# Causal mask of a stick-breaking attention: from an added matmul to the scan's second operand

## The chip, the cores and the metric

The kernel runs on one core of a Trainium2 chip. The metric is the device time of one execution, in microseconds (us); lower is better. A core has five engines, each with its own instruction stream: PE (TensorE, matrix products; its weight loads are listed as PEld), DVE (VectorE), ACT (ScalarE), POOL (GpSimd) and SP (SyncE, which issues most transfers). Each engine works through its own list in order, and an instruction whose operand is not ready holds up all that stand behind it on that engine.

## The reference, cut to what matters

One decoder block on 1024 positions of width 1024. A combined projection feeds three groups of heads (a short convolution, attention, a gated MLP over chunks); their outputs go through an output projection, a squared-ReLU MLP of width 4096 and a gate. The change touches the attention alone: eight heads of width 64, in blocks of 128 queries.

```python
for qb in range(s_len // Q_BLOCK):
    z = jnp.einsum('bqhd,bkhd->bhqk', qi, kj) * scale
    causal = s_pos < t_pos
    log_beta = jax.nn.log_sigmoid(z)
    log_rem = jnp.where(causal, jax.nn.log_sigmoid(-z), 0.0)
    suffix = lax.cumsum(log_rem, axis=3, reverse=True) - log_rem
    weights = jnp.where(causal, jnp.exp(log_beta + suffix), 0.0)
    o = jnp.einsum('bhqk,bkhd->bqhd', weights, vj)
```

With r = sigmoid(-z), and with r taken as 1 at a masked key, the weight of key s is the product of r over the keys after s, less that product taken from s on. So a kernel needs one running product from the last key to the first, and differences of neighbours. A masked key must leave the product at 1.

## The kernel before, in words

Every fp32 product is made of three reduced-precision products. `split` makes a high part (ACT, L138, or L141 with a scale) and a low part (DVE, L139, or L142 with a scale) of an operand, and `product` adds hi·hi, hi·lo and lo·hi in one PSUM bank (L165 to L167).

In the order of PE the block is: the projection of the gated MLP (to 74 us); projection of query, key and value of head pair 0 (`qkv_ps`); attention of head pairs 0 to 3, from 108 us, woven with other work; the output projection (`o_ps`, from 416 us); the MLP up (`f_ps`, from 501 us) and down (`d_ps`, from 816 us); the gate (`g_ps`, to 1205 us).

Attention of a head pair has 8 steps (two heads `hh`, four groups `g` of two query blocks `t`), each in two parts:

- `stick(hh, g)`, for each of two blocks `t` with `W = (t+1)*128` keys: for each half of up to 512 keys, PE makes logits `z` from the queries `QS` by the high and the low part of the keys (`KH` L447, `KL` L449); ACT writes `rem`, the sigmoid of minus the scaled logit (L454). Then DVE runs one scan over the whole row from the last key to the first, in place (L458), and `wt`, the difference of neighbours, is made at L464: on DVE for t = 3, 5, 7, on POOL for the others.
- `gather(hh, g)`: PE transposes `wt` in blocks into `w_tr` (L486), ACT and DVE split it (`wT_hi`, `wT_lo`), PE multiplies by the values `V` into `av` (L504).

In the half that holds the diagonal a third matmul (L453) adds to `z` a constant tile `below`, multiplied by the identity: 0 where the key lies before the query, -2^60 elsewhere. The sigmoid of a masked logit is then 1.

```python
back = rem[:, :W][:, ::-1]
nc.vector.tensor_tensor_scan(out=back, data0=back, data1=back, initial=1.0,
                             op0=ALU.mult, op1=ALU.bypass)
```

The list of steps is written out so that `stick` of the next step comes ahead of `gather` of this one. Both are generators that yield counts (shares of PE work), and `weave` takes from two streams so that their counts grow in proportion: attention of pair `pr` with total `ATTEND`, and, as filler, the projection of pair `pr+1` (`project`) or, with the last pair, the short convolution (`cv_ps`). A projection makes `qkv_ps`, scales query and key (`qk`, L382), and writes `V` (L141, L142). Every second block of queries and keys is then transposed (`turn_qk`: the bank `qk_tr`, L401), and from `qk_tr` come `QS`, its low part `q_lo`, `KH` and, on DVE, two pieces of `KL` (L407). The banks `qk_tr` and `w_tr` come from one pool, `ps_tr`, so a transpose waits until an earlier bank of the pool has been read. After this the framework's scheduler orders each engine's instructions anew, from a timeline that it simulates when it builds the program.

Of the kernel before, what the change touches and what calls it, by code (L numbers as in the profile page):

```python
# [6 lines left out]

F32 = mybir.dt.float32
F32R = mybir.dt.float32r
AF = mybir.ActivationFunctionType  # L10
ALU = mybir.AluOpType
AX = mybir.AxisListType

P = 128
T = 1024
# [17 lines left out]
def hybrid_block(ctx: ExitStack, tc: tile.TileContext, a: dict):  # L33
# [5 lines left out]
    nc = tc.nc  # L39
    PSUM = bass.MemoryType.PSUM  # L40

    const = ctx.enter_context(tc.tile_pool(name="const", bufs=1))
# [61 lines left out]
    for _ in range(WARM):  # L104
        nc.tensor.matmul(warm[:, :P], ones, ones, start=True, stop=True)
    ident_r = const.tile([P, P], F32R, name="ident")
# [1 line left out]
    nc.gpsimd.memset(ident, 0.0)  # L108
    nc.gpsimd.affine_select(out=ident_r, in_=ident, pattern=[[-1, P]], base=0,
                            channel_multiplier=1, compare_op=ALU.not_equal, fill=1.0)  # L110

    below = const.tile([P, P], F32R, name="below")
    nc.gpsimd.memset(below.bitcast(F32), 0.0)
    nc.gpsimd.affine_select(out=below, in_=below.bitcast(F32), pattern=[[-1, P]], base=0,
                            channel_multiplier=1, compare_op=ALU.is_gt, fill=-2.0 ** 60)
    mhalf = const.tile([P, 8], F32, name="mhalf")
    nc.gpsimd.memset(mhalf, -0.5)

# [115 lines left out]
    attn_scope = ExitStack()  # L234
    at = attn_scope.enter_context(tc.tile_pool(name="at", bufs=2))
    lo_p, hi_p = slice(0, HD), slice(HD, P)

# [181 lines left out]
    def attend(pr):  # L421

        QS, KH, KL, V, _ = heads[pr]
        yb = y_kept if pr == 3 else None
        if pr == 3:
            y_kept.extend(halves("y_b"))
        weights, both, seen_g = {}, [None], []

        def store_rows():

            while len(summed) > (0 if pr == 3 else 1):
                to, t = summed.pop(0)
                nc.sync.dma_start(to, t[:HD])

        def stick(hh, g):
            weights[hh, g] = []
            for t in (2 * g, 2 * g + 1):
                W = (t + 1) * P
                th, ts = block(t)

                rem = at.tile([P, T], F32, tag="rem", name=name("rem"), bufs=3)
                wt = at.tile([P, T], F32, tag="wt", name=name("wt"), bufs=4)
                for kh in reversed(range(th + 1)):
                    n = min(HT, W - kh * HT)
                    ks = slice(kh * HT, kh * HT + n)
                    z = bank(ps_z, "z")[:, :n]
                    nc.tensor.matmul(z, QS[hh][th][:, ts], KH[hh][kh][:, :n],  # L447
                                     start=True, stop=False)
                    nc.tensor.matmul(z, QS[hh][th][:, ts], KL[hh][kh][:, :n],  # L449
                                     start=False, stop=kh < th)  # L450
                    if kh == th:

                        nc.tensor.matmul(z[:, n - P:], ident_r, below, start=False, stop=True)  # L453
                    last_act[0] = nc.scalar.activation(rem[:, ks], z, AF.Sigmoid,  # L454
                                                       scale=-HD ** -0.5)

                back = rem[:, :W][:, ::-1]
                nc.vector.tensor_tensor_scan(out=back, data0=back, data1=back, initial=1.0,  # L458
                                             op0=ALU.mult, op1=ALU.bypass)


                on_vector = t in (3, 5, 7)
                nc.gpsimd.memset(wt[:, W - 1:W], 0.0)
                done = (nc.vector if on_vector else nc.gpsimd).tensor_tensor(  # L464
                    out=wt[:, :W - 1], in0=rem[:, 1:W], in1=rem[:, :W - 1], op=ALU.subtract)
                if not on_vector:
                    last_pool[0] = done
                weights[hh, g].append(wt)
                yield 2 * (t + 1) + 10

        def gather(hh, g):
            own = slice(hh * HD, (hh + 1) * HD)
            wts = weights.pop((hh, g))
            av_of[0] ^= 1
            av = av_bank[:, av_of[0] * 256:(av_of[0] + 1) * 256]

            def turn(j):

                tr = bank(ps_tr, "w_tr")
                n = 0  # L480
                parts = []
                for kb in (2 * j, 2 * j + 1):
                    first = 0 if kb <= 2 * g else 1
                    parts.append((kb, n, first))
                    for i in range(first, 2):
                        nc.tensor.transpose(tr[:, n:n + P], wts[i][:, kb * P:(kb + 1) * P], ident)  # L486
                        n += P
                hi, lo = tmp("wT_hi", F32R), tmp("wT_lo", F32R)
                split(tr[:, :n], hi[:, :n], lo[:, :n])
                return parts, hi, lo, n // P  # L490

            turned = []
            for j in range(-2, g + 1):
                if j + 2 <= g:
                    turned.append(turn(j + 2))
                    yield 2 * turned[-1][3] + 10
                if j < 0:
                    continue
                parts, hi, lo, _ = turned.pop(0)
                for kb, o, first in parts:  # L500
                    m = 256 - first * P
                    lhs = V[kb // 2][:, kb % 2, hh].rearrange("p two d -> p (two d)")
                    for part in (hi, lo):
                        nc.tensor.matmul(av[:, first * P:], lhs, part[:, o:o + m],  # L504
                                         start=kb == 0 and part is hi,
                                         stop=kb == 2 * g + 1 and part is lo)
                yield 8

            if yb is None:
                if both[0] is None:  # L510
                    both[0] = slot("y_both")
                t = both[0]
                nc.scalar.copy(t[:, (g % 2) * 256:(g % 2 + 1) * 256], av)
                if len(seen_g) % 2:
                    nc.gpsimd.dma_start(t[:HD], t[HD:], accum_op=ALU.add)
                    summed.append((y_dram[pr, g // 2, own], t))
                    both[0] = None
                seen_g.append(g)
                return
            low = half_tmp("av_lo")  # L520
            nc.scalar.copy(low[:HD], av[HD:])
            nc.vector.tensor_tensor(out=yb[g // 2][own, (g % 2) * 256:(g % 2 + 1) * 256],
                                    in0=av[:HD], in1=low[:HD], op=ALU.add)

        return stick, gather, store_rows

    def attention():
# [19 lines left out]
                yield None  # L547

    AHEAD = 26
    ATTEND = 2 * (72 + 8 * 10 + 72 + 10 * 10 + 80)  # L550


    gs_b = const.tile([P, 256], F32, name="gs_b")
# [144 lines left out]
    fill = stream(project(1), project(2), project(3), convolve())  # L698
# [139 lines left out]
    for q in range(FT):  # L838
        base = 7 * (q - 1)
# [85 lines left out]
    for h in range(2):  # L925
        for n in (0, 4, 1, 5, 2, 6, 3, 7):
# [28 lines left out]
            t = hg[n][h] = late_slot("tmp", "hg")  # L955
# [184 lines left out]
    for s, (c, p, j) in enumerate(steps):  # L1140
# [13 lines left out]
        elif p == 6:  # L1154
            subtract(nc.vector, u_sum[j], u_sum[j], bank)
            if last:
                add(nc.vector, h_res[j][1], h_res[j][1], u_sum[j])
                for h in range(2):
                    t = residual(j + 4, h)
# [185 lines left out]
```

## Time and profile before

| | |
|---|---|
| median of 3 runs | 1213.11 us (1210.53 to 1213.97) |
| the profiled execution | 1212.77 us, its span 1211.1 us |
| granted TensorE clock | 0.995 |
| PE busy | 1188.3 us (98%) |
| DVE busy | 885.2 us (73%) |
| ACT busy | 595.8 us (49%) |
| POOL busy | 405.0 us (33%) |
| mask matmuls (L453) | 64, in the attention |
| scans (L458) | 64, 90.6 us on DVE |

The span is the time from the first to the last instruction, 1.7 us less than the time of that execution. A row of a group of instructions reads: line, engine, operation, output<-inputs, shapes, count, then busy us and mean ns of one, then the engine's idle time just before them and what ended it. A row of the timeline reads: start, length, engine, line, operation, count, and in brackets the idle time ahead with what released it. PE matmuls are pipelined: one begins while the one before it drains, so what a matmul takes from PE is the time from its start to the next start, not its listed length.

### The profile page before, as it was taken

Reading aid. Unit: us, or ns where it says so; the run is one execution under the profiler, and the core shown is the slowest. Engines: PE = TensorE matmul, PEld = TensorE weight load, DVE = VectorE, ACT = ScalarE, POOL = GpSimd, SP = SyncE. Lnnn points to the kernel's source line nnn. Section 1 sums busy time; section 2 is a strip of 40 time slices with the busy share of each in tenths; the row PEclk is TensorE's granted clock in tenths of the full one; section 3 lists DMA queues with packets and bytes.
Section 4 is the critical chain, followed back from the end, with each engine's and each line's share of the span. In section 5 each row is a group of like instructions: output and inputs, shape, how many; then the busy total and the mean of one; then the engine's idle time right before and its main releaser. Section 6 shows DMA issues by size and latency. Waiting matters only on the chain.

```text
span 1211.1 us, 17645 instructions
## 1 busy us (share of the span) xinstructions
PE 1188.3 (98%) x5852; PEld 1015.5 (84%) x5852; DVE 885.2 (73%) x1310; ACT 595.8 (49%) x1148; POOL 405.0 (33%) x472
## 2 busy tenths in 40 slices
PE   9999999999999999999999999999999999999997
PEld 7899899899878888888888888888888888888886
DVE  7846788989887667877877777787665656753597
ACT  7735555565643356734333343355443444546542
POOL 2324435465453312034453544421023301013412
PEclk9999999999999999999999999999999999999999
DMA  9602349989654776779998999677889975644857
GB/s 317 225 18 106 112 152 277 251 176 186 144 117 100 179 265 207 214 189 267 264 251 241 251 244 263 213 258 271 307 261 307 284 260 172 221 155 114 177 162 208
DMA packets 127964, 254.04 MB, mean 210 GB/s; under 512 B 14496, under 2 KB 22432, under 8 KB 127168
## 3 DMA queue, kind: packets, MB, share of 16 engines
q1 hardware_dynamic: 94992, 168.08, 41.5%
q0 software_dynamic: 27664, 57.05, 25.2%
q10 hardware_dynamic: 5216, 27.79, 6.3%
q8 instruction: 46, 0.75, 0.3%
q14 instruction: 46, 0.38, 0.1%
HBM read 192.30 MB, written 92.80 MB: 235 GB/s over the span
## 4 chain that ended last, share of the span: by engine, by line
PE 85%; DVE 7%; DMA 4%; issue 2%; ACT 1%; POOL 0%; ACTq 0%; SPq 0%; DVEq 0%; POOLq 0%
PE f_ps L814 25%; PE d_ps L814 25%; PE g_ps L814 6%; PE qkv_ps L165 3%; PE qkv_ps L166 3%; PE qkv_ps L167 3%; DVE rem L458 2%; PE av L504 2%; PE w_tr L486 2%; PE vu_ps L167 1%; PE vu_ps L165 1%; PE vu_ps L166 1%; PE o_ps L167 1%; PE o_ps L165 1%; PE o_ps L166 1%
## 5 line engine op out<-in xcount | busy, mean ns | idle before, releaser
L139 DVE TENSOR_TENSOR w_lo<-raw,w_hi 128x512 fp32r<-128x512 f32 x280 | 240.8, 864 | 87.4 <-ACT w_hi L138 85.5
L138 ACT CAST w_hi<-raw 128x512 fp32r<-128x512 f32 x280 | 172.0, 619 | 241.1 <-PE d_ps L814 121.0
L814 PE MATMUL f_ps<-hn_hi,w_hi 128*128 128x512 f32 x448 | 175.1, 392 | 0.0
L814 PE MATMUL f_ps<-hn_hi,w_lo 128*128 128x512 f32 x448 | 174.9, 391 | 0.0
L814 PE MATMUL f_ps<-hn_lo,w_hi 128*128 128x512 f32 x448 | 174.8, 390 | 0.0
L814 PE MATMUL d_ps<-f_hi,w_hi 128*128 128x512 f32 x448 | 174.8, 390 | 0.0
L814 PE MATMUL d_ps<-f_hi,w_lo 128*128 128x512 f32 x448 | 174.3, 389 | 0.0
L814 PE MATMUL d_ps<-f_lo,w_hi 128*128 128x512 f32 x448 | 174.3, 389 | 0.0
L458 DVE TENSOR_TENSOR_SCAN rem<-rem 128x128 f32<-128x128 f32 (+3 forms) x64 | 90.6, 1426 | 19.3 <-ACT rem L454 19.2
L814 PEld LDWEIGHTS f_ps<-hn_hi,w_hi 128*128 128x128 f32 x448 | 84.5, 189 | 17.8 <-issue 0.2
L814 PEld LDWEIGHTS f_ps<-hn_lo,w_hi 128*128 128x128 f32 x448 | 84.5, 189 | 17.7 <-issue 0.2
L814 PEld LDWEIGHTS f_ps<-hn_hi,w_lo 128*128 128x128 f32 x448 | 84.4, 188 | 17.8
L814 PEld LDWEIGHTS d_ps<-f_lo,w_hi 128*128 128x128 f32 x448 | 84.1, 188 | 17.8 <-issue 0.2
L814 PEld LDWEIGHTS d_ps<-f_hi,w_hi 128*128 128x128 f32 x448 | 84.1, 188 | 17.6 <-issue 0.2
L814 PEld LDWEIGHTS d_ps<-f_hi,w_lo 128*128 128x128 f32 x448 | 84.1, 188 | 17.5
L165 PE MATMUL qkv_ps<-whi,xn_hi 128*128 128x384 f32 x256 | 89.7, 350 | 1.1 <-DVE V L142 1.1
L167 PE MATMUL qkv_ps<-whi,xn_lo 128*128 128x384 f32 x256 | 87.6, 342 | 0.0
L166 PE MATMUL qkv_ps<-wlo,xn_hi 128*128 128x384 f32 x256 | 87.4, 341 | 0.0
L139 DVE TENSOR_TENSOR f_lo<-raw,f_hi 128x512 fp32r<-128x512 f32 x112 | 77.1, 718 | 9.6 <-ACT f_hi L138 9.3
L800 POOL TENSOR_TENSOR S<-S,sq 128x512 f32<-128x512 f32 x19 | 27.4, 1441 | 157.8 <-ACT sq L876 157.8
L138 ACT CAST f_hi<-raw 128x512 fp32r<-128x512 f32 x112 | 67.0, 620 | 23.3 <-DMA raw<-f_dram 20.0
L454 ACT ACTIVATE rem<-z 128x128 f32<-128x128 f32 (+3 forms) x96 | 46.4, 500 | 33.0 <-PE z L453 19.2
(252 smaller groups left out, 2656.2 us busy)
## 6 DMA issues: line engine op xcount, KB each, us to landing
raw<-in_w_ff SPq DMA_DIRECT2D x148, 256.0 KB, 4.0
raw<-f_dram SPq DMA_DIRECT2D x112, 256.0 KB, 4.9
raw<-w_sums SPq DMA_DIRECT2D x64, 256.0 KB, 4.1
f_dram<-f SPq DMA_DIRECT2D x48, 256.0 KB, 4.1
f_dram<-t SPq DMA_DIRECT2D x48, 256.0 KB, 3.8
w_sums<-in_w_ff POOLq DMA_DIRECT2D x8, 1024.0 KB, 12.5
w_sums<-w_sums POOLq DMA_DIRECT2D x8, 1024.0 KB, 13.1
raw<-in_w_out SPq DMA_DIRECT2D x28, 256.0 KB, 3.3
```

Source lines behind the costliest of these rows:

```text
L138: last_hi[0] = nc.scalar.copy(hi, src)
L139: low.tensor_tensor(out=lo, in0=src, in1=hi, op=ALU.subtract)
L165: nc.tensor.matmul(ps, lh, rh, start=first and i == 0, stop=False)
L166: nc.tensor.matmul(ps, lh, rl, start=False, stop=False)
L167: done = nc.tensor.matmul(ps, ll, rh, start=False, stop=last and i == len(terms) - 1)
L454: last_act[0] = nc.scalar.activation(rem[:, ks], z, AF.Sigmoid, scale=-HD ** -0.5)
L458: nc.vector.tensor_tensor_scan(out=back, data0=back, data1=back, initial=1.0, op0=ALU.mult, op1=ALU.bypass)
L486: nc.tensor.transpose(tr[:, n:n + P], wts[i][:, kb * P:(kb + 1) * P], ident)
L504: nc.tensor.matmul(av[:, first * P:], lhs, part[:, o:o + m], start=kb == 0 and part is hi, stop=kb == 2 * g + 1 and part is lo)
L800: return eng.tensor_tensor(out=out, in0=x, in1=y, op=ALU.add)
L814: done = nc.tensor.matmul(bank, l, r, start=first and k == 0 and i == 0, stop=k == len(b) - 1 and i == 2, skip_group_check=True)
```

## The change

The mask leaves the logits. The tile `below`, its two POOL instructions and the matmul at L453 go, and the matmul with `KL` closes the bank. In their place stands a tile `after` of 8-bit integers, 128 by 1024, with 1 in the last 128 columns where the key does not lie before the query, and 0 elsewhere. The scan takes its last `W` columns, reversed, as second operand: the running value is multiplied by `rem`, then the larger of that and the mask is taken. A masked key gives 1 whatever its logit, and at other keys the larger of a product of sigmoids and 0 is the product itself. The counts that `stick` yields fall by 2 for each block (what the mask matmul had counted), and `ATTEND` from 808 to 776.

```diff
-    below = const.tile([P, P], F32R, name="below")
-    nc.gpsimd.memset(below.bitcast(F32), 0.0)
-    nc.gpsimd.affine_select(out=below, in_=below.bitcast(F32), pattern=[[-1, P]], base=0,
-                            channel_multiplier=1, compare_op=ALU.is_gt, fill=-2.0 ** 60)
...
+    after = at.tile([P, T], INT8, name="after", bufs=1)
+    nc.gpsimd.memset(after, 0.0)
+    nc.gpsimd.affine_select(out=after[:, T - P:], in_=after[:, T - P:], pattern=[[-1, P]], base=0,
+                            channel_multiplier=1, compare_op=ALU.is_gt, fill=1.0)
...
                     nc.tensor.matmul(z, QS[hh][th][:, ts], KL[hh][kh][:, :n],
-                                     start=False, stop=kh < th)
-                    if kh == th:
-
-                        nc.tensor.matmul(z[:, n - P:], ident_r, below, start=False, stop=True)
+                                     start=False, stop=True)
                     last_act[0] = nc.scalar.activation(rem[:, ks], z, AF.Sigmoid,
                                                        scale=-HD ** -0.5)
                 back = rem[:, :W][:, ::-1]
-                nc.vector.tensor_tensor_scan(out=back, data0=back, data1=back, initial=1.0,
-                                             op0=ALU.mult, op1=ALU.bypass)
+                nc.vector.tensor_tensor_scan(out=back, data0=back,
+                                             data1=after[:, T - W:][:, ::-1], initial=1.0,
+                                             op0=ALU.mult, op1=ALU.max)
...
-                yield 2 * (t + 1) + 10
+                yield 2 * (t + 1) + 8
...
-    ATTEND = 2 * (72 + 8 * 10 + 72 + 10 * 10 + 80)
+    ATTEND = 2 * (72 + 8 * 8 + 72 + 10 * 10 + 80)
```

The counts and the simulated timeline move instructions on every engine. Lines 139, 142, 382, 407, 414 to 416, 447, 449 and 458 of before are lines 135, 138, 384, 409, 416 to 418, 448, 450 and 457 of the changed kernel; 464, 486 and 504 stay. The numbers behind names are given anew in each program. The rows call a scan SCALAR_TENSOR_TENSOR.

The first place is in the second half of head pair 0. On DVE before (the 128x1024 scan of `rem_1725` belongs to the first block with 1024 keys of the second head; both `KL` rows read the bank `qk_tr_1680`):

```order
L458 SCALAR_TENSOR_TENSOR rem_1610<-rem_1610 128x1024
L139 TENSOR_TENSOR wT_lo_1659<-w_tr_1654,wT_hi_1658 128x384
L464 TENSOR_TENSOR wt_1611<-rem_1610 128x1023
L142 SCALAR_TENSOR_TENSOR q_lo_1411<-qk_tr_1680,c_gq,QS_1410 128x256
L382 TENSOR_TENSOR qk_1713<-qkv_ps_1718,rs_1793 128x256
L458 SCALAR_TENSOR_TENSOR rem_1692<-rem_1692 128x896
L458 SCALAR_TENSOR_TENSOR rem_1725<-rem_1725 128x1024
L407 SCALAR_TENSOR_TENSOR KL_1405<-qk_tr_1680,c_gk,KH_1409 64x256
L407 SCALAR_TENSOR_TENSOR KL_1407<-qk_tr_1680,c_gk,KH_1409 64x256
```

And on DVE now (`rem_1716` is the same scan, `qk_tr_1672` the same bank):

```order
L457 SCALAR_TENSOR_TENSOR rem_1586<-rem_1586,after 128x1024
L138 SCALAR_TENSOR_TENSOR q_lo_1410<-qk_tr_1672,c_gq,QS_1409 128x256
L384 TENSOR_TENSOR qk_1704<-qkv_ps_1709,rs_1783 128x256
L464 TENSOR_TENSOR wt_1587<-rem_1586 128x1023
L457 SCALAR_TENSOR_TENSOR rem_1684<-rem_1684,after 128x896
L409 SCALAR_TENSOR_TENSOR KL_1404<-qk_tr_1672,c_gk,KH_1408 64x256
L409 SCALAR_TENSOR_TENSOR KL_1406<-qk_tr_1672,c_gk,KH_1408 64x256
L138 SCALAR_TENSOR_TENSOR V_1706<-qkv_ps_1609,r_569,V_1706 128x2x64
L138 SCALAR_TENSOR_TENSOR V_1706<-qkv_ps_1709,r_569,V_1706 128x2x64
L457 SCALAR_TENSOR_TENSOR rem_1716<-rem_1716,after 128x1024
```

The two `KL` rows, and two of `V`, have moved ahead of the longest scan. On PE at the same place before, up to the first transpose into a bank that `KL` must have left:

```order
L453 MATMUL z_1845<-below,ident 128x128
L447 MATMUL z_1850<-KH_957,QS_1159 128x512
L449 MATMUL z_1850<-KL_951,QS_1159 128x512
L504 MATMUL av_87<-wT_hi_1750,V_992 128x256
L447 MATMUL z_1865<-KH_1160,QS_1159 128x256
L449 MATMUL z_1865<-KL_1154,QS_1159 128x256
L453 MATMUL z_1865<-below,ident 128x128
L447 MATMUL z_1870<-KH_957,QS_1159 128x512
L449 MATMUL z_1870<-KL_951,QS_1159 128x512
L486 MATMUL w_tr_1775<-ident,wt_1580 128x128
```

On PE there now:

```order
L448 MATMUL z_1839<-KH_957,QS_1159 128x512
L450 MATMUL z_1839<-KL_951,QS_1159 128x512
L504 MATMUL av_87<-wT_hi_1740,V_992 128x256
L448 MATMUL z_1854<-KH_1160,QS_1159 128x256
L450 MATMUL z_1854<-KL_1154,QS_1159 128x256
L486 MATMUL w_tr_1765<-ident,wt_1568 128x128
```

The masks are gone, and the last two logit matmuls of the block (`z_1870` before) have moved behind the transposes.

The second place is in head pair 1, on DVE before (`wT_lo_2790` is a low part that PE needs for its next product with `V`):

```order
L464 TENSOR_TENSOR wt_2753<-rem_2752 128x767
L139 TENSOR_TENSOR wT_lo_2790<-w_tr_2784,wT_hi_2789 128x512
L407 SCALAR_TENSOR_TENSOR KL_2271<-qk_tr_2766,c_gk,KH_2275 64x256
L407 SCALAR_TENSOR_TENSOR KL_2273<-qk_tr_2766,c_gk,KH_2275 64x256
L414 COPY QS_2278<-QS_2276 64x512
L415 COPY QS_2278<-q_lo_2277 64x512
L139 TENSOR_TENSOR wT_lo_2818<-w_tr_2812,wT_hi_2817 128x512
L142 SCALAR_TENSOR_TENSOR V_2802<-qkv_ps_2686,r_731,V_2802 128x2x64
L416 COPY QS_2276<-q_lo_2277 64x512
L377 TENSOR_REDUCE ss_2875<-qk_sq_2872 128x4
L458 SCALAR_TENSOR_TENSOR rem_2891<-rem_2891 128x384
```

On DVE there now (`wT_lo_2762` is `wT_lo_2790` of before, `rem_2863` is `rem_2891`):

```order
L135 TENSOR_TENSOR wT_lo_2676<-w_tr_2671,wT_hi_2675 128x384
L457 SCALAR_TENSOR_TENSOR rem_2863<-rem_2863,after 128x384
L138 SCALAR_TENSOR_TENSOR q_lo_2263<-qk_tr_2738,c_gq,QS_2262 128x256
L384 TENSOR_TENSOR qk_2772<-qkv_ps_2660,rs_2770 128x256
L135 TENSOR_TENSOR wT_lo_2762<-w_tr_2756,wT_hi_2761 128x512
L409 SCALAR_TENSOR_TENSOR KL_2257<-qk_tr_2738,c_gk,KH_2261 64x256
L409 SCALAR_TENSOR_TENSOR KL_2259<-qk_tr_2738,c_gk,KH_2261 64x256
```

A scan and a `qk` now stand ahead of that low part.

The third place is in head pair 3, on DVE before (`rem_4338` is a scan over 1024 keys, `cv_u` belongs to the convolution):

```order
L139 TENSOR_TENSOR wT_lo_4367<-w_tr_4361,wT_hi_4366 128x512
L650 TENSOR_TENSOR cv_u_3999<-cv_ps_4304,cv_u_3999 128x512
L139 TENSOR_TENSOR wlo_4906<-stage_4903,whi_4905 128x384
L139 TENSOR_TENSOR wT_lo_4382<-w_tr_4376,wT_hi_4381 128x512
L458 SCALAR_TENSOR_TENSOR rem_4338<-rem_4338 128x1024
L139 TENSOR_TENSOR wT_lo_4421<-w_tr_4415,wT_hi_4420 128x512
L464 TENSOR_TENSOR wt_4339<-rem_4338 128x1023
```

On DVE there now:

```order
L457 SCALAR_TENSOR_TENSOR rem_4281<-rem_4281,after 128x1024
L135 TENSOR_TENSOR wT_lo_4309<-w_tr_4303,wT_hi_4308 128x512
L650 TENSOR_TENSOR cv_u_3949<-cv_ps_4248,cv_u_3949 128x512
L135 TENSOR_TENSOR wlo_4842<-stage_4839,whi_4841 128x384
L464 TENSOR_TENSOR wt_4282<-rem_4281 128x1023
L135 TENSOR_TENSOR wT_lo_4324<-w_tr_4318,wT_hi_4323 128x512
L135 TENSOR_TENSOR wT_lo_4363<-w_tr_4357,wT_hi_4362 128x512
```

The scan has moved ahead of the low part of the first transposed block, so it no longer stands between the two low parts that PE needs one after the other.

More of the change, by code (lines that the diff above doesn't have):

```diff
@@ L9 @@
 F32R = mybir.dt.float32r
+INT8 = mybir.dt.int8
 AF = mybir.ActivationFunctionType
```

## The prediction

> **What bounds the kernel now.** I read the page first (share of each engine, chain, costliest groups), then busy time in windows over the attention, then PE's groups and waits there, and last the timeline where PE waits. The page's span, PE row, chain by engine and scan group:
>
> ```profile
> span 1211.1 us, 17645 instructions
> PE 1188.3 (98%) x5852; PEld 1015.5 (84%) x5852; DVE 885.2 (73%) x1310; ACT 595.8 (49%) x1148; POOL 405.0 (33%) x472
> ...
> PE 85%; DVE 7%; DMA 4%; issue 2%; ACT 1%; POOL 0%; ACTq 0%; SPq 0%; DVEq 0%; POOLq 0%
> ...
> L458 DVE TENSOR_TENSOR_SCAN rem<-rem 128x128 f32<-128x128 f32 (+3 forms) x64 | 90.6, 1426 | 19.3 <-ACT rem L454 19.2
> ```
>
> PE is the bound, and DVE holds 7% of the chain. Windows show where; columns are window and length, busy us of PE, PEld, DVE, ACT, POOL with counts, granted clock, DMA share, GB/s:
>
> ```profile
> 100.00:140.00 40.00, 38.69 (x242) 37.98 (x240) 27.89 (x51) 23.28 (x58) 18.18 (x24) 1.00 0.45 151
> 140.00:160.00 20.00, 15.67 (x87) 13.66 (x86) 19.69 (x22) 9.35 (x24) 9.86 (x7) 0.91 0.29 106
> 160.00:220.00 60.00, 58.11 (x391) 55.92 (x390) 50.68 (x80) 37.44 (x94) 31.39 (x48) 1.00 0.75 200
> 220.00:260.00 40.00, 39.05 (x264) 37.68 (x263) 38.05 (x58) 23.12 (x58) 22.75 (x33) 1.00 0.92 226
> 260.00:280.00 20.00, 20.00 (x131) 19.48 (x131) 15.83 (x25) 11.54 (x29) 10.14 (x15) 1.00 1.00 195
> 280.00:320.00 40.00, 38.93 (x254) 36.25 (x254) 38.71 (x65) 24.26 (x59) 20.55 (x29) 1.00 0.80 161
> 320.00:400.00 80.00, 78.58 (x437) 66.11 (x436) 60.01 (x80) 33.76 (x70) 31.98 (x40) 1.00 0.59 129
> 416.00:1205.00 789.00, 786.23 (x3504) 650.58 (x3504) 556.97 (x775) 367.88 (x631) 222.69 (x224) 1.00 0.79 234
> ```
>
> In four windows DVE has slack and PE is nearly full. In three (140 to 160, 220 to 260, 280 to 320) DVE is busy 19.69 of 20, 38.05 of 40 and 38.71 of 40 us: there it shares the bound. After 416 us PE is busy 786.23 of 789, so what the attention saves moves the end of the program by as much.
>
> **The mask matmul.** PE's group in 100 to 400 us, the start of the attention on PE, and where the masks lie (the same line in the three windows full of DVE):
>
> ```profile
> L453 PE MATMUL z<-below,ident 128*128 128x128 f32 x64 | 15.3, 239 | 0.0
> ...
> 108.84 0.27 PE L449 MATMUL z<-KL,QS 128*128 128x128 f32 x1
> 108.95 0.27 PE L453 MATMUL z<-below,ident 128*128 128x128 f32 x1
> 109.06 0.33 PE L447 MATMUL z<-KH,QS 128*128 128x256 f32 x1
> ...
> 109.35 0.23 PE L453 MATMUL z<-below,ident 128*128 128x128 f32 x1
> 109.41 0.40 PE L401 MATMUL qk_tr<-ident,qk 128*128 128x128 f32 x2
> ...
> 140.00:160.00 20.00, 1.19 (x5) 0.83 (x5) 0.91 0.29 106
> 220.00:260.00 40.00, 2.10 (x9) 1.70 (x9) 1.00 0.92 226
> 280.00:320.00 40.00, 2.29 (x9) 1.71 (x9) 1.00 0.80 161
> ```
>
> The 239 ns are pipelined length. From start to next start the first mask takes 109.06 - 108.95 = 0.11 us, the second 109.41 - 109.35 = 0.06; it also holds back its neighbours, since L449 to L453 is 0.11 where 128 columns alone could take 0.06. So a mask is worth 0.06 to 0.16 us (0.11 + 0.05). I take 0.11, the slot that the first shows, since most masks stand before a matmul with other weights as it does: 64 x 0.11 = 7.0 us (3.8 to 10.2). [...]
>
> Of the 64, 5 + 9 + 9 = 23 stand where DVE is full; 41 x 0.11 = 4.5 us come off PE where PE alone is bound. Of the 23 (2.5 us) I count half, 1.25 us: PE waits only at a few points there, and masks between two waits that DVE ends are lost, those after the last are won. Ends: 0 and 2.5.
>
> **The longer scan.** It now reads `rem` and the mask. Its forms, and its total beside all of DVE in the three full windows (two rows of sums):
>
> ```profile
> L458 DVE TENSOR_TENSOR_SCAN rem<-rem 128x1024 f32<-128x1024 f32 x8 | 21.1, 2638 | 0.0
> ...
> L458 DVE TENSOR_TENSOR_SCAN rem<-rem 128x128 f32<-128x128 f32 x8 | 3.3, 416 | 4.1 <-ACT rem L454 4.1
> sum 100.00, DVE 38.16; mean DVE 12.72
> sum 100.00, PE 93.65 PEld 87.59 DVE 96.46 ACT 56.73 POOL 53.16; mean PE 31.22 PEld 29.20 DVE 32.15 ACT 18.91 POOL 17.72
> 360.26 2.27 DVE L458 TENSOR_TENSOR_SCAN rem<-rem 128x1024 f32<-128x1024 f32 x1
> 221.36 3.21 DVE L458 TENSOR_TENSOR_SCAN rem<-rem 128x1024 f32<-128x1024 f32 x1
> 220.75 1.68 POOL L464 TENSOR_TENSOR wt<-rem 128x895 f32<-128x895 f32 x1 [2.93 <-DVE rem L458]
> ```
>
> No scan before has another tile, 8-bit, as second operand. (2638 - 416) / 896 = 2.5 ns per element in the mean, 2.27 us for 1024 undisturbed. The same scan took 3.21 when POOL was reading from 220.75 to 222.43: it started at 221.36, and 3.21 less the overlap of 1.07 leaves 2.14. So the old scan, with its unused second operand, already waits for POOL. Two operands are addressed before and after, with fewer bytes after. Ends: -10% (a narrower operand helps) and +40% (3.21 / 2.27, every scan meeting POOL once more); I take 0, the undisturbed row being nearest.
>
> [...]
>
> **Orders moved.** Beginning with head pair 0's burst, the waits of PE over the whole attention that bear on it, then the rows:
>
> ```profile
> PE av L504 <- DVE wT_lo L139: 3.1, 4, 0.9
> PE w_tr L486 <- DVE KL L407: 2.8, 2, 2.0
> 147.59 4.19 DVE L458 TENSOR_TENSOR_SCAN rem<-rem 128x896 f32<-128x896 f32 x2
> 151.70 0.97 DVE L407 SCALAR_TENSOR_TENSOR KL<-qk_tr,c_gk,KH 64x256 fp32r<-64x256 f32 x2
> 152.70 0.61 DVE L142 SCALAR_TENSOR_TENSOR V<-qkv_ps,r,V 128x128 fp32r<-128x128 f32 x2
> ...
> 152.73 0.44 PE L486 MATMUL w_tr<-ident,wt 128*128 128x128 f32 x2 [1.98 <-DVE KL L407]
> ```
>
> DVE ran two scans (896 and 1024 keys) from 147.59, then `KL`, and PE stood still for 1.98 us until `KL` had emptied the bank. Now `KL` precedes the second scan, so it comes 2.2 us earlier (half of 4.19 and a little, 2.27 at most) and this wait ends. What is late next is that scan: two `V` splits (0.61 us in all) also pass it, so the weights from it come later by 0.97 + 0.6 = 1.6 us, for the following transposes. I credit 1.4 of the 1.98; ends 0 and 1.98.
>
> Head pair 1: a 384-key scan, 1.0 us (half of the first row below), now precedes the low part that ran at 233.14. PE's next product waits at 236.28 for a later low part already, and DVE has the scan behind it by then. I charge 0.6; ends 0 and 1.0.
>
> ```profile
> 237.31 2.06 DVE L458 TENSOR_TENSOR_SCAN rem<-rem 128x384 f32<-128x384 f32 x2
> 233.14 0.68 DVE L139 TENSOR_TENSOR wT_lo<-w_tr,wT_hi 128x512 fp32r<-128x512 f32 x1
> 236.28 0.38 PE L504 MATMUL av<-wT_lo,V 128*128 128x256 f32 x1 [0.95 <-DVE wT_lo L139]
> 363.17 0.38 PE L504 MATMUL av<-wT_lo,V 128*128 128x256 f32 x1 [0.87 <-DVE wT_lo L139]
> ```
>
> Head pair 3: the scan of 2.27 us at 360.26 stood ahead of the low part for which PE waited 0.87 us at 363.17. It now stands ahead of the convolution's work, so I credit 0.7 (0 to 0.87). Elsewhere small moves of `V`, `qk` and `wt` go both ways; I charge 0.3 for new waits (-1 to +2). The two POOL instructions of `after` replace two at the program's start; the first scan is over 100 us away, so they cost nothing unless the early transfers queued behind them on POOL are late, which would show before 20 us. The later activations now wait for `KL`'s matmul and not for the mask: that is the same 0.11 us, not counted again.
>
> **The sum:** -4.5 - 1.25 + 0 - 1.4 + 0.6 - 0.7 + 0.3 = -6.95. Against the profiled execution, 1212.8 us (its span of 1211.1 and 1.7 around it), that is 1205.8, so 1206. The median of the runs is 1213.1, 0.3 us above that execution, inside their spread.
>
> **Rivals.**
>
> A, the forecast: PE's slots come off and mostly stay off; 1203 to 1209.
>
> B: DVE sets the ends of its three windows and gives little back, and the new orders cost as much as they save. Then only the 41 masks at the lower price hold, 41 x 0.06 = 2.5 us, 1210.3. For it: DVE at 96.46 of 100 us there. Against it: the two places of 1.98 and 0.87, where the order itself made the wait.
>
> C, slower: the 8-bit second operand slows the scan, by conversion or by longer waits for POOL's reads. Scans are 38.16 us of the three full windows, so it takes 18% (6.95 / 38.16) to undo the gain and 28% to show as slower; at +40% it is 15.3 - 6.95 = +8.3, 1221. Against it: the scan already takes over 2 ns an element with two addressed operands, and already meets POOL.
>
> D: more. The half-clock stretch goes too:
>
> ```profile
> 150.00:154.00 4.00, 2.02 (x13) 1.57 (x12) 3.94 (x7) 1.15 (x3) 3.25 (x1) 1.00 0.00 0
> 154.00:158.00 4.00, 4.00 (x16) 4.00 (x15) 4.00 (x4) 0.64 (x2) 0.00 (x0) 0.57 1.20 442
> ```
>
> After PE was busy 2.02 of 4 us it ran at 0.57 of its clock for the next 4, that is 4 x 0.43 = 1.7 us lost. If the 1.98 us wait shrinks, this may not occur, and with masks at 0.14 the sum is near -11: 1202. [...]
>
> **How the numbers follow.** A 0.64, B 0.16, C 0.07, D 0.13. A tenth of the range's misses I leave below and a tenth above: low 1201 is D's middle less 1, high 1212 takes in B whole. A measurement of this kernel tells a change from none at about 0.3%, 3.6 us: faster is below 1209.5, slower above 1216.7. Faster: nearly all of A and D, a little of B, 0.77; slower: most of C, 0.06; the rest, 0.17, within.
>
> **What would show it.** Right: 64 fewer PE matmuls; PE busy down by about 7 us in 100 to 400; scans still near 90 us; the waits `w_tr` on `KL` (2.8) under 1.5; o_ps starting 6 to 8 us earlier, and nothing gained after it. Wrong: scans above 100 us (C); new waits of `av` on `wT_lo` above 5 us in all (B); a wait of PE before 20 us.

## Result, and the profile after

The changed kernel took 1206.67 us (median of 4 runs, 1206.52 to 1208.23) against 1213.22; the ratio is 0.9949, with a 95% interval of 0.9929 to 0.9968. Timed once more with the experiments it took 1208.98 us against 1213.21, 0.9967 (0.9955 to 0.9978). The medians differ by 6.6 and by 4.2 us. The profiled execution took 1206.75 us. Its page, in the parts shown of before (span, busy time, chain by engine, scan group):

```profile
span 1205.0 us, 17538 instructions
...
PE 1181.0 (98%) x5788; PEld 1007.1 (84%) x5788; DVE 885.7 (73%) x1310; ACT 595.5 (49%) x1148; POOL 400.5 (33%) x472
...
PE 88%; DVE 8%; ACT 1%; issue 1%; DMA 1%; POOL 1%; SPq 0%; DVEq 0%; ACTq 0%; POOLq 0%
...
L457 DVE TENSOR_TENSOR_SCAN rem<-rem,after 128x128 f32<-128x128 f32 (+3 forms) x64 | 90.9, 1431 | 13.3 <-ACT rem L452 13.3
```

PE has 64 matmuls less and 7.3 us less busy time (1188.3 to 1181.0). The span fell by 6.1. The scans went from 90.6 to 90.9 us, so the 8-bit operand costs nothing. PE's waits between 100 and 420 us after (who waits for whom, us in total, times, longest):

```profile
PE w_tr L486 <- DVE KL L409: 3.6, 4, 1.5
PE w_tr L486 <- DVE wt L464: 3.2, 3, 1.6
PE av L504 <- DVE wT_lo L135: 2.9, 4, 1.8
PE qk_tr L403 <- DVE qk L384: 1.5, 1, 1.5
PE qkv_ps L161 <- DVE V L138: 0.8, 2, 0.5
PE av L504 <- DVE y_b L522: 0.5, 1, 0.5
PE w_tr L486 <- DVE wT_lo L135: 0.3, 1, 0.3
```

They add up to 12.8 us. Before, the same view adds up to 11.3; its two longest rows stand in the prediction (`av` on `wT_lo` 3.1, `w_tr` on `KL` 2.8), the others are:

```profile
PE qk_tr L401 <- DVE qk L382: 1.3, 1, 1.3
PE qkv_ps L165 <- DVE V L142: 1.1, 1, 1.1
PE av L504 <- ACT wT_hi L138: 0.9, 1, 0.9
PE w_tr L486 <- DVE wt L464: 0.8, 1, 0.8
PE o_ps L165 <- DVE cv_acc L663: 0.5, 1, 0.5
PE av L504 <- DVE y_b L522: 0.4, 1, 0.4
PE z L447 <- ACT rem L454: 0.4, 2, 0.2
```

So PE gave up the masks, but waits longer. By stretch of the attention, from the same view in windows:

| stretch | waits before | waits after | forecast |
|---|---|---|---|
| head pair 0, first half | 1.3 | 1.8 | small |
| burst of head pair 0 (138 to 154 us before) | 4.3 | 3.0 | -1.4 |
| up to head pair 1 | 1.1 | 1.8 | small |
| head pair 1 | 1.7 | 2.5 | +0.6 |
| head pair 2 | 1.0 | 3.2 | small |
| start of head pair 3 | 0.4 | 0.5 | small |
| end of head pair 3 and start of `o_ps` | 1.4 | 0.0 | -0.7 |

The burst on PE and DVE after (timeline):

```profile
147.02 0.88 PE L486 MATMUL w_tr<-ident,wt 128*128 128x128 f32 x6 [1.64 <-DVE wt L464]
...
149.93 0.63 PE L486 MATMUL w_tr<-ident,wt 128*128 128x128 f32 x4 [0.94 <-DVE KL L409]
...
148.82 0.97 DVE L409 SCALAR_TENSOR_TENSOR KL<-qk_tr,c_gk,KH 64x256 fp32r<-64x256 f32 x2
...
150.34 2.52 DVE L457 TENSOR_TENSOR_SCAN rem<-rem,after 128x1024 f32<-128x1024 f32 x1
```

`KL` precedes the long scan, and the wait of 1.98 us for it became 0.94. A new one of 1.64 us for `wt` stands ahead of it, which the forecast did not have.

Head pair 2 shows where slots went. Before, then after, each with the subtraction that lets PE begin six transposes, these transposes, and the next four, which wait for `KL`:

```profile
281.68 1.22 DVE L464 TENSOR_TENSOR wt<-rem 128x1023 f32<-128x1023 f32 x1
...
285.06 0.97 DVE L407 SCALAR_TENSOR_TENSOR KL<-qk_tr,c_gk,KH 64x256 fp32r<-64x256 f32 x2
...
282.95 0.87 PE L486 MATMUL w_tr<-ident,wt 128*128 128x128 f32 x6
...
286.08 0.66 PE L486 MATMUL w_tr<-ident,wt 128*128 128x128 f32 x4 [0.84 <-DVE KL L407]
```

```profile
278.27 1.21 DVE L464 TENSOR_TENSOR wt<-rem 128x1023 f32<-128x1023 f32 x1
...
281.65 0.97 DVE L409 SCALAR_TENSOR_TENSOR KL<-qk_tr,c_gk,KH 64x256 fp32r<-64x256 f32 x2
...
279.54 0.88 PE L486 MATMUL w_tr<-ident,wt 128*128 128x128 f32 x6 [0.66 <-DVE wt L464]
...
282.77 0.63 PE L486 MATMUL w_tr<-ident,wt 128*128 128x128 f32 x4 [1.54 <-DVE KL L409]
```

From the first transposes to the next four is 286.08 - 282.95 = 3.13 us before and 282.77 - 279.54 = 3.23 after. DVE does the same between `wt` and `KL`, a scan of 896 keys (2.02 us before and after) and `qk` (0.40), and that is what lasts. On PE two mask matmuls and one block of logits less stand in between, and the wait grew by 1.54 - 0.84 = 0.7 us. By the starts on PE before, the two masks held it for 0.18 and 0.22 us and the logits, which now run ahead of the transposes, for 0.26. So the 0.4 us of the masks turned into waiting here.

A third quantity is the granted clock. Stretches of the span run at half clock (0.50 from 518 to 520 us below), each losing 1.7 us in these profiles (in the prediction's row, 4 us at 0.57). Before had one at 154 and one at 522 us. The changed kernel's profile has one, and the profile of the same program in the repeated run has none there:

```profile
516.00:518.00 2.00, 2.00 (x10) 1.68 (x11) 2.00 (x5) 0.00 (x0) 0.88 (x1) 0.88 0.61 155
518.00:520.00 2.00, 2.00 (x6) 1.54 (x6) 2.00 (x4) 0.00 (x0) 0.87 (x2) 0.50 0.88 262
520.00:522.00 2.00, 2.00 (x9) 1.61 (x8) 1.45 (x4) 0.62 (x1) 0.55 (x1) 0.77 0.91 297
```

```profile
516.00:518.00 2.00, 2.00 (x18) 1.95 (x18) 2.00 (x4) 0.00 (x0) 0.00 (x0) 1.00 0.00 0
518.00:520.00 2.00, 2.00 (x10) 1.64 (x9) 2.00 (x5) 0.00 (x0) 1.40 (x1) 1.00 0.81 270
520.00:522.00 2.00, 2.00 (x10) 1.65 (x9) 2.00 (x4) 0.62 (x1) 0.90 (x1) 1.00 0.90 283
```

The first three windows lose 2 x (0.12 + 0.50 + 0.23) = 1.7 us. Such stretches come and go between executions of one program, and they go with much of the spread of its runs: of the 35 runs of the kernel before in the first set of experiments, the 15 with a granted clock of 0.996 or more have a median of 1212.1 us, the 9 with 0.994 or less one of 1215.7.

### The profile page after: what moved, and what is told of

Its sections match the earlier page's. It is cut to its first block, busy times and chain, and to the rows that moved or that the text cites. A ratio compares the mean times of both kernels' runs of the same rounds, so it can differ in the third digit from the quotient of the medians.

```text
span 1205.0 us, 17538 instructions
## 1 busy us (share of the span) xinstructions
PE 1181.0 (98%) x5788; PEld 1007.1 (84%) x5788; DVE 885.7 (73%) x1310; ACT 595.5 (49%) x1148; POOL 400.5 (33%) x472
## 4 chain that ended last, share of the span: by engine, by line
PE 88%; DVE 8%; ACT 1%; issue 1%; DMA 1%; POOL 1%; SPq 0%; DVEq 0%; ACTq 0%; POOLq 0%
PE f_ps L814 25%; PE d_ps L814 25%; PE g_ps L814 6%; DVE rem L457 3%; PE qkv_ps L161 3%; PE qkv_ps L162 2%; PE qkv_ps L163 2%; PE o_ps L161 2%; PE o_ps L163 2%; PE o_ps L162 2%; PE av L504 2%; PE cv_ps L163 2%; PE cv_ps L161 2%; PE cv_ps L162 2%; PE w_tr L486 1%; PE vu_ps L162 1%
## 5 line engine op out<-in xcount | busy, mean ns | idle before, releaser
L457 DVE TENSOR_TENSOR_SCAN rem<-rem,after 128x128 f32<-128x128 f32 (+3 forms) x64 | 90.9, 1431 | 13.3 <-ACT rem L452 13.3
L134 ACT CAST f_hi<-raw 128x512 fp32r<-128x512 f32 x112 | 67.1, 620 | 25.6 <-DMA raw<-f_dram 21.6
L800 POOL TENSOR_TENSOR S<-S,sq 128x512 f32<-128x512 f32 x19 | 25.6, 1347 | 160.1 <-ACT sq L876 160.1
```

The source lines that it names most:

```text
L134: last_hi[0] = nc.scalar.copy(hi, src)
L457: nc.vector.tensor_tensor_scan(out=back, data0=back, data1=after[:, T - W:][:, ::-1], initial=1.0, op0=ALU.mult, op1=ALU.max)
L800: return eng.tensor_tensor(out=out, in0=x, in1=y, op=ALU.add)
```

## The experiments

The theories: 1, each mask holds a slot of PE of about 0.11 us, and removing it shows in the time; 2, masks were hidden and the new counts made the gain; 3, the gain is the half-clock stretch that went; 4 (after the first four runs), slots are real, but DVE sets the pace in stretches, so PE waits more when they go, and how much depends on the order drawn.

The profiles of twelve kernels in one ledger. The time is the median of the runs; the columns from the span on are of the one execution that was profiled. Waits are the sum of PE's waits between 100 and 425 us. Half-clock loss is the sum of 2 x (1 - granted clock) over windows of 2 us whose clock is under 0.97, without the last 25 us, in which the clock falls to half behind the last matmul (0.50 from 1206 to 1212 us in the kernel before). The rest is the span less both.

| kernel | masks | time, us | ratio to before (interval) | span | waits | half-clock loss | rest |
|---|---|---|---|---|---|---|---|
| before | 64 | 1213.1 | | 1211.1 | 11.3 | 3.3 | 1196.5 |
| changed | 0 | 1206.7 | 0.9949 (0.9929 to 0.9968) | 1205.0 | 12.8 | 1.7 | 1190.5 |
| changed, again | 0 | 1209.0 | 0.9967 (0.9955 to 0.9978) | 1204.9 | 12.8 | 0.0 | 1192.1 |
| no masks, old counts | 0 | 1212.4 | 0.9991 (0.9976 to 1.0005) | 1209.4 | 15.9 | 1.7 | 1191.8 |
| masks, new counts | 64 | 1215.5 | 1.0015 (0.9999 to 1.0031) | 1216.2 | 12.0 | 6.8 | 1197.4 |
| masks and scan operand | 64 | 1214.0 | 0.9993 (0.9976 to 1.0009) | 1210.0 | 11.0 | 3.4 | 1195.6 |
| masks twice | 128 | 1214.3 | 1.0008 (0.9993 to 1.0023) | 1211.8 | 6.1 | 3.4 | 1202.3 |
| changed, 64 late slots | 64 late | 1214.8 | 1.0016 (1.0003 to 1.0028) | 1212.9 | 13.2 | 0.0 | 1199.7 |
| no masks, counts +6 | 0 | 1212.7 | 0.9992 (0.9979 to 1.0004) | 1211.8 | 15.2 | 6.8 | 1189.8 |
| relief, no masks | 0 | 1217.5 | 1.0034 (1.0021 to 1.0046) | 1215.9 | 18.4 | 6.8 | 1190.7 |
| relief, masks | 64 | 1228.2 | 1.0123 (1.0105 to 1.0142) | 1225.4 | 18.7 | 10.2 | 1196.5 |
| no masks, later turn | 0 | 1208.0 | 0.9948 (0.9928 to 0.9968) | 1206.4 | 10.0 | 6.8 | 1189.6 |

The rest lies between 1189.6 and 1192.1 for the six profiles without masks (mean 1190.8), between 1195.6 and 1197.4 for the four with 64 in the attention (mean 1196.5), and is 1202.3 with 128. So 64 masks are 5.7 and then 5.8 us of slots, 0.09 us each. Waits and half-clock losses explain what else differs, to 1.3 us. With the waits of the whole span in place of this window the two steps are 5.2 and 6.5 us, and the rests of equal kernels lie within 1.8 us of their mean.

From the second set of runs on, the expectations count waits in a wider way that no view here gives: 17.2 and 20.5 us where the ledger has 12.8 (changed) and 15.9 (old counts). So their bounds on waits lie about 4.5 us above the ledger's.

**The second operand alone.**

```diff
-    nc.vector.tensor_tensor_scan(out=back, data0=back, data1=back, initial=1.0,
-                                 op0=ALU.mult, op1=ALU.bypass)
+    nc.vector.tensor_tensor_scan(out=back, data0=back, data1=after[:, T - W:][:, ::-1],
+                                 initial=1.0, op0=ALU.mult, op1=ALU.max)
```

> The kernel before with the scan's second operand added (8-bit mask, max) and the mask matmuls kept; the order of the engines is nearly that of before. If the second operand costs nothing: 1212 to 1214.5 us, scans 90 to 92 us in all. If it slows the scan, hidden so far behind the gain on PE: scans over 95 us and 1216 us or more.

It measured 1213.97, within the interval of no change. Only 12 of 5638 PE rows moved against before, and the scans took, as before, 90.6 us:

```profile
L464 DVE TENSOR_TENSOR_SCAN rem<-rem,after 128x128 f32<-128x128 f32 (+3 forms) x64 | 90.6, 1427 | 19.2 <-ACT rem L460 19.2
```

The operand is free. That falls out as a cause on either side.

**Masks without the counts, and counts without the masks.** The first is the changed kernel with

```diff
-                yield 2 * (t + 1) + 8
+                yield 2 * (t + 1) + 10
...
-    ATTEND = 2 * (72 + 8 * 8 + 72 + 10 * 10 + 80)
+    ATTEND = 2 * (72 + 8 * 10 + 72 + 10 * 10 + 80)
```

and the second the kernel before with the same two lines turned round.

> The changed kernel with the old counts (+10 for each block and ATTEND 808): no mask matmul, mask in the scan, the two streams woven as before. Theory 1 (each mask matmul holds a slot of PE of about 0.11 us, and the counts matter little): 1205 to 1209 us. Rival 2 (the masks were hidden and the gain came from the new weave): 1211 to 1215 us. Rival 3 (the gain is the lost half-clock stretch): this depends on its trace; with a stretch at half clock inside the attention about 1208.5, without one about 1206.5.

> The kernel before with the new counts alone (+8 and 776); the mask matmuls stay. Theory 1: 1211 to 1215 us, the order worth 2 us at most either way. Rival 2: 1205 to 1208 us. Rival 3: 1.7 us lower than before only if the trace shows no half-clock stretch inside the attention.

They measured 1212.44 and 1215.49: neither part alone is a gain. Theory 1 in its plain form failed on the first (1205 to 1209 expected), where theory 2 had the time, and by 0.5 us on the second; theory 2 failed on the second (1205 to 1208). Theory 3 doesn't hold for the first either: its profile has one half-clock stretch, as the changed kernel's has, and is 4.4 us longer. The ledger tells what is different. Without masks but with the old counts PE waits 15.9 us instead of 12.8, most of it at one kind of place:

```profile
PE av L504 <- DVE wT_lo L135: 5.1, 7, 1.8
PE w_tr L486 <- DVE KL L409: 3.6, 4, 1.5
PE w_tr L486 <- DVE wt L464: 3.1, 3, 1.6
PE qkv_ps L161 <- DVE V L138: 2.7, 4, 1.6
```

Against the changed kernel `av` on `wT_lo` is up from 2.9 to 5.1 and `V` from 0.8 to 2.7, the other two are equal. The extra `wT_lo` waits lie at the end of head pair 3 (363 to 371 us), the place of the third order shown above: with the old counts DVE runs a scan of 3.42 us (from 359.23) and a weight's split ahead of the first of these low parts (a wait of 1.3 us), and `wt` ahead of the next one for which PE waits (0.8 us). The counts with masks drew an order with 12.0 us of waits, but its profile lost 6.8 us at half clock.

**The changed kernel again,** beside the others:

> The changed kernel itself, timed again beside the others. If the old counts really cost it some 5 us (waits of PE on DVE of 20.5 us in the attention against 17.2, and more half-clock stretches): 1205.5 to 1208.5 us. If its first runs were only lucky in the half-clock stretches: 1210 to 1213 us.

At 1208.98 it stands just outside the first range and nearer to it than to the second; the gain is real, 4.2 us here and 6.6 at first, with intervals that overlap.

**Masks twice.**

```diff
-    nc.tensor.matmul(z[:, n - P:], ident_r, below, start=False, stop=True)
+    nc.tensor.matmul(z[:, n - P:], ident_r, below, start=False, stop=False)
+    nc.tensor.matmul(z[:, n - P:], ident_r, below, start=False, stop=True)
```

> The kernel before with every mask matmul issued twice (128 in all; a masked logit is then lower by 2^60 once more, and its sigmoid is 1 as before). Theory 1: 64 more slots, 4 us (0.06 each) to 10 us (0.16 each), likeliest 7: 1217 to 1223 us. Rival 2 (masks hidden): 1212 to 1215 us.

It measured 1214.3, only 1 us over before, where theory 1 expected 7; the time is in rival 2's range. The slots are there, but PE's waits are nearly halved:

```profile
PE w_tr L487 <- DVE KL L407: 3.3, 3, 1.3
PE z L447 <- ACT rem L455: 2.4, 3, 0.9
PE qk_tr L401 <- DVE qk L382: 0.2, 1, 0.2
PE w_tr L487 <- DVE wt L465: 0.2, 1, 0.2
```

5.8 us more in the rest and 11.3 - 6.1 = 5.2 us less waiting. Its order was drawn anew (283 of 5637 rows moved), so what part of the 5.2 is the order's and what part the fuller PE's is not separated.

**The price of a slot by itself.** 64 extra matmuls of a zero tile, in the MLP up stage, on the changed kernel:

```diff
+                if k == 1 and i == 2 and extra[0] < 64:
+                    extra[0] += 1
+                    nc.tensor.matmul(bank[:, :P], ident_r, zero, start=False, stop=False,
+                                     skip_group_check=True)
```

> The changed kernel with 64 extra 128x128 matmuls of a zero tile in the first 64 blocks of the MLP up stage, where PE runs without waits; the order of the engines is kept. Theories 1 and 4 both: 64 x 0.11 = 7 us over the changed kernel (4 to 10). If a matmul of 128 columns with other weights costs less in a full stream (0.06): 4 us.

1214.84 us, 5.9 over the changed kernel's median in the same set of runs. The two profiles had no half-clock stretch before the end, and their spans differ by 1212.9 - 1204.9 = 8.0 us, 0.125 us each. PE was busy without a break there (group, window of the stage, and one of the 64 with what follows it):

```profile
L824 PE MATMUL f_ps<-zero,ident 128*128 128x128 f32 x64 | 14.2, 223 | 0.0
...
500.00:816.00 316.00, 316.00 (x1434) 262.27 (x1433) 236.57 (x283) 125.43 (x214) 124.88 (x113) 1.00 0.85 239
...
505.98 0.22 PE L824 MATMUL f_ps<-zero,ident 128*128 128x128 f32 x1
506.04 0.45 PE L820 MATMUL f_ps<-hn_hi,w_hi 128*128 128x512 f32 x1
506.33 0.40 PE L820 MATMUL f_ps<-hn_lo,w_hi 128*128 128x512 f32 x1
506.56 0.39 PE L820 MATMUL f_ps<-hn_hi,w_lo 128*128 128x512 f32 x1
```

From its start to the second start behind it are 506.33 - 505.98 = 0.35 us, where a matmul of 512 columns alone takes 506.56 - 506.33 = 0.23. So the slot is 0.12 us: 0.06 of its own, and 0.06 by which its neighbour's grows. The medians' 5.9 us are less, 0.09 each, with other executions and their half-clock stretches in them. The order was kept (4 PE rows moved). Here, where nothing waits, a slot cost its full price, 0.12 us; this is theory 1's number in the place where theory 1 is complete.

**The order as it is written,** without rearrangement from a simulated timeline, before and without masks (old counts in both):

```diff
-    with tile.TileContext(nc, schedule_with_timeline_sim=True) as tc:
+    with tile.TileContext(nc, schedule_with_timeline_sim=False) as tc:
```

> The kernel before, with each engine's instructions left nearly in the order in which the program is written (no rearrangement from a simulated timeline). It is the partner of the next kernel; it should be slower than the kernel before, 1215 to 1260 us, since rows meant to overlap are no longer interleaved.

> The same with the mask in the scan and without the mask matmuls, old counts: against its partner only 74 of 5638 PE rows are moved. Theory 1 (slots of PE, nothing hidden): 6 to 8 us below its partner. Theory 4 (DVE sets the pace in stretches of the attention, so PE waits longer where masks are gone): 1 to 4 us below it, with PE's waits in the attention longer by 3 to 6 us.

1295.81 and 1295.69 us: no difference, and far above the 1215 to 1260 expected of the first. I had expected 1 to 8 between them. PE's busy time fell from 1220.4 to 1214.8, by 5.6 us. Here the attention runs to 463 us and later stages wait too, so the ledger is taken over the whole span (1294.6 and 1296.1 us): waits rose from 66.2 to 73.3 us, the half-clock loss from 25.6 to 27.2, and the rest fell from 1202.8 to 1195.6. The span's +1.5 us is -7.2 in the rest, +7.1 in waits and +1.6 at half clock. Of the waits 4.9 us are in the attention (42.0 to 46.9 between 100 and 465 us), within theory 4's 3 to 6. So the slots came off here too, and waits took all of it; taking out the masks bought nothing.

**Another weave without masks.** The changed kernel with `+ 6` and `8 * 6` in the place of `+ 8` and `8 * 8`:

> The changed kernel with still smaller counts (+6 for each block, ATTEND 744): a third weave without masks, some 138 of 5637 PE rows moved. Theory 4 (the masks' slots are won only as far as the order leaves DVE ahead of PE, so the time goes by the waits of the order drawn): waits of PE on DVE in the attention between 14 and 22 us and the time with them, 1205 to 1213 us. Rival (smaller counts are right by themselves, as the mask's work is gone): the same or better than with +8, 1204 to 1208 us.

1212.72 us. Smaller counts are not right by themselves. One wait, which ends at 155.3 us, takes most of what the masks gave, and two half-clock stretches (154 to 161 us) follow its beginning:

```profile
PE w_tr L486 <- DVE wT_lo L135: 4.8, 2, 4.5
```

**DVE relieved,** with and without masks: `on_vector = t == 7` for `t in (3, 5, 7)`, so 16 more differences go to POOL.

> The changed kernel with DVE relieved: the difference of neighbours for t = 3 and t = 5 is made on POOL too, so 16 subtractions (0.74 and 1.0 us each, some 14 us of DVE) leave DVE. Theory 4: with DVE less often the bound, waits of PE on DVE fall below 14 us (17.2 now), time 1203 to 1208 us. Rival 5 (what PE waits for is the order of single rows, and POOL's longer subtraction comes later): waits 17 us or more, 1209 to 1214 us.

> The kernel before, masks and old counts, with the same relief of DVE. It is the partner of the run with relief and no masks. Theory 4: with DVE relieved the masks are no longer hidden, so this kernel is 6 to 9 us above its partner, at 1211 to 1215 us. Rival 5: the difference stays at 3 to 6 us.

1217.51 and 1228.15 us. The relief failed at what it was to do: DVE's busy time fell by 7.7 us (885.7 to 878.0 without masks), not by some 14 as expected, and waits rose to 18.4 and 18.7 us, so of the first kernel rival 5 had the waits right and a time still too low. That rows come later from POOL, as rival 5 says, is not shown: none of PE's waits ends at POOL directly, the largest end at `wT_lo`. The difference of the pair, 10.6 us, is beyond both theories' ranges. The spans differ by 9.5 us. In the ledger the waits are nearly equal and the masks show in full, 1196.5 - 1190.7 = 5.8 us in the rest, with 10.2 - 6.8 = 3.4 more at half clock. But the kernel with masks still waits behind the ledger's window: over the whole span its waits are 23.6 us against 21.5, and 4.0 us are left for the rest.

**A later turn of query and key:** 90 for 72 in `later(72, lambda t=t, qk=qk: turn_qk(heads[pr], t, qk))`.

> The changed kernel with the transposes of query and key (turn_qk) emitted 90 instead of 72 units of work after their projection, at which PE waits 1.5 us for qk and 3.6 us for KL in the changed kernel. If those waits are set by how soon PE reaches the transposes: the wait on qk goes, waits of PE on DVE in the attention 14 to 16 us in all, 1204 to 1208 us. If any new order only moves the waits (the ledger of slots, waits and half-clock stretches): waits 16 to 21 us, 1207 to 1213 us, and span less waits less half-clock losses between 1185.5 and 1188.

1208.02 us, ratio 0.9948, at the upper end of the first range and no better than the changed kernel. The waits on `qk` and `KL` are gone, as the first theory has it, but the transposes `qk_tr` now wait 1.3 us for `wT_lo`:

```profile
PE av L504 <- DVE wT_lo L135: 4.2, 5, 1.9
PE qkv_ps L161 <- DVE V L138: 2.0, 2, 1.8
PE w_tr L486 <- DVE wT_lo L135: 1.3, 1, 1.3
PE qk_tr L403 <- DVE wT_lo L135: 1.3, 1, 1.3
```

10.0 us of waits in all are 2.8 less than in the changed kernel; in the profile four half-clock stretches' worth, 6.8 us, took that back. No version was found that is clearly better than the changed kernel.

## Why the prediction was right, and where not

The time (1206, measured 1206.67 and 1208.98) lies in the range, and the mechanism of A is there. The sum came out by luck in part: two terms missed in opposite directions, the new waits (0.3 for 3.5 us) and the half clock (0 for -1.6), and others have the right number by another way than was said.

- **64 slots at 0.11 us, half of those under a full DVE lost: -5.75.** The rest of the ledger gives 5.7 for 64 masks, 0.09 each in the attention and 0.125 in a stage without waits. The number agrees by luck, the reasoning less: by the ledger a slot is smaller than 0.11, none is lost, and what DVE took back came as longer waits, not as masks that cannot be won.
- **The scan's operand: 0.** Right, in the changed kernel (90.9 us) and alone (90.6). The end of -10% for a narrower operand was the author's guess, and nothing shows it. A scan that lasts longer beside POOL is seen once more before: the one at 346.87 us took 3.82 us, with POOL's `cv_u` (L651) over 1.66 of it, which leaves 2.16. But the row of 2.27 us at 360.26, taken as undisturbed, had a `cv_u` over its whole length; there POOL's took longer, 3.66 us against 1.83 at 346.70. Two scans of 1024 keys that had only MEMSETs and DMA issues of POOL beside them (212.94 and 278.76 us) took 2.29.
- **Burst of head pair 0: -1.4.** Measured 4.3 to 3.0, -1.3. The wait on `KL` halved and did not end; a wait of 1.6 on `wt` came, and those on `wT_lo` and `wT_hi` shrank from 2.1 to 0.5. So the row named gave 1.0 of the 1.4, and the other parts nearly cancel.
- **Head pair 1: +0.6.** Measured +0.8, but not where it was forecast: the wait of `av` for `wT_lo` at 236.28 (0.95 us) went instead of growing, and waits on `KL` (1.1) and `V` (0.5) came. The agreement is luck.
- **End of head pair 3: -0.7.** Measured -1.4, of it 0.9 from `wT_lo` and 0.5 from the start of `o_ps`.
- **"I charge 0.3 for new waits."** This step failed. Outside the three named places waits grew by 0.5 + 0.7 + 2.2 + 0.1 = 3.5 us, above the bound of +2 given for it. Head pair 2 alone has 2.2; of these 1.4 are at the place shown above (0.84 to 0.66 + 1.54), where DVE runs the same rows between `wt` and `KL` and PE has less to do.
- **The half clock.** The sum had nothing for it; rival D did. The changed kernel's profile lost 1.7 us less than that of before. So the span's -6.1 is -6.0 in the rest (1196.5 to 1190.5), +1.5 in waits and -1.6 at half clock.

Rival B was half right: DVE does set the pace, and with other orders of the same change (old counts, +6) it takes nearly everything back, 1212.4 and 1212.7. The prediction gave the counts no term of their own, and they decide whether the slots are kept. Of what was to show it: PE's busy time fell by 7.3 us over the span, but by 2.4 in the window of 100 to 400 us that was named (289.0 to 286.7), since the changed kernel is some us ahead at its end and runs other work there; `w_tr` on `KL` under 1.5 us was wrong (3.6); `o_ps` starts 5.5 us earlier (416.17 to 410.71), just short of 6, and behind it 0.6 us more was gained.

## What to carry to other kernels

A matmul's slot was a fair price where the stage has no waits (0.12 us in the MLP up stage); where another engine is nearly full, measure PE's waits and not only its busy time, for here work taken off PE came back as waiting (7.1 of 7.2 us in the order as written). In a kernel whose order is drawn from counts and a simulated timeline, every edit draws a new order, and a new order here was worth 3.4 to 6 us (1212.4 and 1212.7 against 1206.7 to 1209.0, all without masks), as much as the edit; so an edit is to be timed under several orders before it is called good or bad. A ledger of slots, waits and half-clock losses, one row for each profile, separates the three.

## What the runs showed of the hardware

The half-clock stretches were not expected to matter so much. They lose 1.7 us each or twice that (3.4 us from 152 to 160 us with masks and new counts), and the profiles have from none to the worth of six in kernels of about equal length. The same program had one at 516 us in one execution and none in another. Those in the attention go with idle time of PE: for thirteen of them in the ledger's profiles (one of 3.4 us counted once) PE was busy for only 0.00 to 1.27 of 2 us in the window in which the clock first falls or in the one before, as behind the 1.98 us at 150.75 in the kernel before, and in the 4.5 us wait above. A wait alone did not always bring one: some 1.8 us at 120 to 122 us in the kernel with counts +6 were followed by a stretch, 1.76 us that ended at 121.43 us in the changed kernel by none. The one near 520 us, in 7 of the 12 profiles of the ledger, follows no wait of PE, but 24 matmuls of 2 columns one behind another (513.59 to 516.18 us in the changed kernel); that these set it off is an inference and was not tried, and the repeated run of the changed kernel has the same 24 (16 and 18 matmuls in its windows at 514 and 516 us, 10 in the next) at a granted clock of 1.00.

```profile
513.59 0.28 PE L889 MATMUL ms_ps<-ones,S 128*128 128x2 f32 x2
...
515.73 0.59 PE L889 MATMUL ms_ps<-ones,sq 128*128 128x2 f32 x4
516.18 0.49 PE L814 MATMUL f_ps<-hn_hi,w_hi 128*128 128x512 f32 x1
```
